# S5 blocks without zero halves, and products on 64x64 quarters of TensorE, in a hybrid layer

## Chip, cores and metric

One core of a Trainium2 chip runs the whole program. The metric is the device time of one execution in microseconds (us), median of several runs; lower is better.

## The reference

One layer on 512 positions of width 1024, all in float32. A normalised input goes through one projection `w_in`, whose columns feed three token mixers: A, sparse attention that keeps 128 keys a query; B, the S5 state space branch; C, a gated delta rule. Each is gated, projected and merged; then follow an output projection, a gated MLP with a short convolution and a last norm. The change lies in B alone:

```python
ab = exp(dt * (a_re + 1j * a_im))            # 32 groups x 64 states; here in complex form
bb = (ab - 1) / a * (b_re + 1j * b_im)       # 64 states x 16 channels a group
x  = einsum('tgm,gpm->tgp', u, bb)           # u: 512 positions, 32 groups of 16 channels
h[t] = ab * h[t-1] + x[t]
y  = einsum('tgp,gmp->tgm', h.re, c_re) - einsum('tgp,gmp->tgm', h.im, c_im) + d * u
y  = gelu(y);  y = y * sigmoid(y @ w_glu)
```

## The kernel before

**Chunks.** The sequence is cut in 128 chunks of 4 positions. For a group, its 16 channels by 4 positions j make 64 rows; two groups make a pair, so a pair's input is 128 rows by 128 chunks. `s5_uu` (L583) loads this input, U, from a copy `s_ud` in DRAM: a tile [128, 8, 128] for each half hf of 8 pairs, by 16 DMAs on SP's queue with 16 partitions each (L592).

**Tables.** `s5_setup` (L369) works out the powers of ab and bb on DVE, ACT and POOL. `s5_half` (L463), called for each half, builds the matrices of 8 pairs:
- `blocks` (L477 to L482) makes a tile of 128 x 8 x 128 and lets POOL set two of its quarters to zero (L480, L481): the blocks of a pair stand on the diagonal, since the groups don't mix.
- The B blocks (b4blk; L491 to L495), real and imaginary: a product u1 on DVE, a product u2 on POOL, and two combines of 64 partitions x 512 on DVE (L495), one for each group.
- kt (L501, L502): 16 products for 8 pairs, block x C with 16 columns moving. Transposes (L509) of the blocks, four to a PSUM bank, and copies by ACT (L510) give WT, which takes the input to the chunk's state.
- The CA blocks (cablk; L519 to L523) are made like the B blocks. kt and d give ks (L529, L530), which a product with the selection `selt` (L535) and two ACT copies (L539) turn into T, the part of the output that comes from the same chunk.
- The tables of cos and sin for the scan follow (L555 to L576).

**Steps.** `s5_main` (L596) then runs for each set of 4 pairs a state step A (`s5_state`, L647: 8 products WT x U into two banks `pt`, then a chain on DVE with two scans, which gives sr and si) and an output step B (`s5_out`, L692: 12 products T x U, CA0 x sr, CA1 x si into one bank `po`, gelu on ACT and DVE, and 8 DMAs of 16 partitions into `s_yd`, L715). The order is A0 A1 B0 A2 B1 A3 B2 B3. After these it loads the GLU weights (tiles glw), reads y back (yT, L618) and multiplies (L633 to L635).

**Helpers.** `mm` (L246) and `tr` (L249) record every product and transpose, so one line stands for all, and the tile names tell them apart. PSUM has the tags acc (2 banks), sm (2), pt (3) and po (1). `wload` (L271) brings 512 KB of weights (tile w, two buffers) through SP's queue, lets ACT cast the high part wh (L254) and DVE (L255), or for each third POOL (L284), subtract the low part wl; `dense` (L289) multiplies hh x wh, hl x wh and hh x wl. A float32 product of the program shows as two MATMUL and two LDWEIGHTS records, a transpose as one.

**Order.** S5 is a generator that yields between its parts. It is woven with a filler of projections (top-k part of A and the gates, in an order written out by hand) at a rate R_S5, and a scheduler then orders the instructions of each engine:

```python
fill = _order(ORD, {"t": tk, "g": gt})
drain(_weave(_chain(setup, self.s5_main()), fill, R_S5))
```

Of the kernel before, what the change touches and what calls it, by code (L numbers as in the profile page):

```python
# [50 lines left out]
def _consts():  # L51
# [25 lines left out]
    for g in range(2):  # L77
        for m in range(16):
            dm[g * 64 + 48 + m, m] = 1.0
# [9 lines left out]
def _layout(inp):  # L89
# [34 lines left out]
    pp("d", np.repeat(d, 4, 2).transpose(1, 2, 3, 0))  # L124
# [48 lines left out]
R_S5 = 1.075  # L173
R_QKV = 0.606
# [49 lines left out]
class _K:  # L224
# [238 lines left out]
    def s5_half(self, hf):  # L463
# [6 lines left out]
        dims = [128, 8, 4, 16]  # L470
        fl2 = lambda e: e.rearrange("p a b c d -> p a (b c d)")

        def b2t(nm):
            t = self.s5e.tile(dims, F32, tag="s2", name="s5_" + nm, bufs=2)
            return t

        def blocks(tag):  # L477
            e = (self.s5e if tag == "b4" else q).tile([128, 8, 2, 4, 16], F32, tag=tag, name="s5_" + tag + "blk", bufs={"b4": 4, "ca": 4, "T": 2}[tag])
            with self.tc.issue_after(self.lastp.ins):
                nc.gpsimd.memset(e[0:64, :, 1], 0.0)  # L480
                nc.gpsimd.memset(e[64:128, :, 0], 0.0)  # L481
            return e  # L482

        b4 = lambda a: _bc(a[:, sl], 2, 4)

        a4 = lambda a: _bc(a[:, sl, 3::-1], 3, 16)
        es = []
        for (x1, y1, x2, y2, op) in ((ar, bb[0], ai, bb[1], OP.subtract), (ar, bb[1], ai, bb[0], OP.add)):
            e = blocks("b4")
            u1, u2 = b2t("u1"), b2t("u2")  # L490
            tt(u1, a4(x1), b4(y1), OP.mult)  # L491
            (nc.gpsimd.tensor_tensor if 'u' in PO else tt)(u2, a4(x2), b4(y2), OP.mult)
            for g in range(2):
                s = slice(g * 64, g * 64 + 64)
                tt(e[s, :, g], u1[s], u2[s], op)  # L495
            es.append(e)
        cre3 = v3("cre")
        kt = self.acc("sm")
        for i in range(8):
            ko = kt[:, i * 16:i * 16 + 16]  # L500
            self.mm(ko, fl2(es[0])[:, i], cre3[:, hf * 8 + i], True, False)  # L501
            self.mm(ko, fl2(es[1])[:, i], cin[:, hf * 8 + i], False, True)  # L502
        WT = []
        for ri in range(2):
            w = q.tile([128, 8, 128], F32, tag="wt", name="s5_wt", bufs=4)
            for c in range(2):
                ps = self.acc("sm")
                for i in range(4):
                    self.tr(ps[:, i * 128:(i + 1) * 128], fl2(es[ri])[:, c * 4 + i])  # L509
                nc.scalar.copy(w[:, c * 4:c * 4 + 4].rearrange("p a b -> p (a b)"), ps)  # L510
            WT.append(w)
        yield 1

        a4 = lambda a: _bc(a[:, sl, 1:5], 3, 16)
        CA = []
        for ri, (y1, y2) in enumerate(((cre3, cin), (cin, cre3))):
            e = blocks("ca")
# [13 lines left out]
        T = blocks("T")  # L531
# [4 lines left out]
        pv = ps.rearrange("p (t a b) -> p a t b", t=4, a=8)  # L536
        for g in range(2):
            s = slice(g * 64, g * 64 + 64)
            nc.scalar.copy(T[s, :, g], pv[s])  # L539
# [55 lines left out]

    def s5_main(self):  # L596
        nc = self.nc
        self.yd = self.dp.tile([512, 512], F32, tag="yd", name="s5_yd", bufs=1)
        self.yyh, self.yyl, self.s5s_ = [], [], [None] * 4
# [3 lines left out]
        for st in ("A0", "A1", "B0", "A2", "B1", "A3", "B2", "B3"):  # L603
            qq = self.s5q[int(st[1])]
            if st[0] == "A":
                self.s5s_[int(st[1])] = self.s5_state(*qq)
            else:
                self.s5_out(*(qq[:5] + self.s5s_[int(st[1])]))
            yield 1
# [37 lines left out]
    def s5_state(self, hf, o, WT, CA, T, cosT, sinT, m4):  # L647
# [6 lines left out]
        pr_, pi_ = self.acc("pt"), self.acc("pt")  # L654
        for i in range(4):
# [36 lines left out]
    def s5_out(self, hf, o, WT, CA, T, sr, si):  # L692
        nc, q = self.nc, self.s5
        tt = nc.vector.tensor_tensor
        yv = self.yd.rearrange("(a g m) (t c) -> g t m a c", g=2, m=16, t=4)
        v = lambda x: x.rearrange("p (a c) -> p a c", a=4)
        qq = hf * 2 + o // 4
        U = self.U[hf]
        py = self.acc("po")
        for i in range(4):  # L700
            c = slice(i * 128, (i + 1) * 128)
            self.mm(py[:, c], T[:, o + i].rearrange("p g t m -> p (g t m)"), U[:, o + i], True, False)
            self.mm(py[:, c], CA[0][:, o + i], sr[:, i, 0:128], False, False)
            self.mm(py[:, c], CA[1][:, o + i], si[:, i, 0:128], False, True)
        s = q.tile([128, 512], F32, tag="b2", name="s5_gs", bufs=self.nb2)
        yy = q.tile([128, 512], F32, tag="b2", name="s5_yy", bufs=self.nb2)
        nc.scalar.activation(s, py, AF.Square)
        nc.vector.tensor_scalar(s, s, 0.044715, 1.0, OP.mult, OP.add)
        tt(s, s, py, OP.mult)
        nc.scalar.activation(s, s, AF.Tanh, scale=math.sqrt(2.0 / math.pi))  # L710
        nc.vector.scalar_tensor_tensor(yy, s, 1.0, py, OP.add, OP.mult)
# [911 lines left out]
```

## Time and profile before

| | |
|---|---|
| median of 3 runs | 957.44 us (954.11 to 960.42) |
| the profiled execution | 964.91 us |
| its span | 963.1 us, mean granted clock 0.981 |
| PE busy | 929.9 us (97%), 4572 records |
| DVE busy | 661.4 us (69%) |
| ACT, POOL busy | 418.2 us (43%), 138.6 us (14%) |

The span is the profiler's, from the first instruction to the last, and lies 1.8 us under that execution's time. Times in views are us from the span's start. Busy times of PE count overlapping records of pipelined products, so the time that a product costs is the distance of starts. S5's matrices are built from about 50 to 135 us and its steps run from 100 to 210 us, with the filler between them; the delta rule and the attention follow, and from some 600 us on the MLP.

### The profile page before, as it was taken

How to read it: one execution, taken by the hardware profiler on the slowest of the kernel's cores; microseconds unless marked ns; L12 is line 12 of the kernel's file. 1: busy time of each engine (PE TensorE's matmuls, PEld its weight loads, DVE VectorE, ACT ScalarE, POOL GpSimd, SP SyncE). 2: the span in 40 equal slices, each digit the busy share in tenths (PEclk: the TensorE clock that was granted, in tenths of full speed). 3: DMA queues.
4: the chain of work that ended last, by engine and by line, in shares of the span. 5: the costliest groups of instructions: out<-in, count | busy, mean ns of one | idle time of the engine just before them, and what ended most of it. 6: DMA issues, size and time to landing. Idle time of an engine off the chain costs nothing. (4 is left out here: it accounts for less than half of the span.)

```text
span 963.1 us, 12377 instructions
## 1 busy us (share of the span) xinstructions
PE 929.9 (97%) x4572; PEld 765.1 (79%) x4572; DVE 661.4 (69%) x1108; ACT 418.2 (43%) x751; POOL 138.6 (14%) x136
## 2 busy tenths in 40 slices
PE   7989999999999999899999999999999999999997
PEld 5668788788888787688867788988888888888885
DVE  5999779969998779436767746676766667622423
ACT  6455353335665643127861424444444443421312
POOL 3473403111123411302112000000000000000000
PEclk9999999999999999889999999999999999999999
DMA  8352513463224645523007542333232322223222
GB/s 317 123 154 88 141 67 100 151 186 108 87 91 116 175 120 164 152 69 141 23 23 241 187 173 73 125 97 100 89 109 88 107 90 94 103 88 110 88 65 88
DMA packets 54445, 113.49 MB, mean 118 GB/s; under 512 B 16240, under 2 KB 20720, under 8 KB 54384
## 3 DMA queue, kind: packets, MB, share of 16 engines
q1 hardware_dynamic: 52304, 109.28, 34.9%
q0 software_dynamic: 2080, 3.41, 1.9%
q8 instruction: 36, 0.59, 0.3%
q14 instruction: 25, 0.20, 0.1%
HBM read 94.84 MB, written 14.42 MB: 113 GB/s over the span
## 5 line engine op out<-in xcount | busy, mean ns | idle before, releaser
L255 DVE TENSOR_TENSOR wl<-w,wh 128x1024 fp32r<-128x1024 f32 (+1 forms) x121 | 147.8, 1222 | 130.8 <-ACT wh L254 130.6
L254 ACT CAST wh<-w 128x1024 fp32r<-128x1024 f32 (+1 forms) x121 | 125.3, 1036 | 187.5 <-PE ps_acc L246 80.9
L246 PE MATMUL ps_acc<-hh,wh 128*128 128x512 f32 x376 | 152.2, 405 | 4.7 <-ACT wh L254 2.9
L246 PE MATMUL ps_acc<-hh,wl 128*128 128x512 f32 x376 | 151.4, 403 | 3.3 <-DVE wl L255 3.3
L246 PE MATMUL ps_acc<-hl,wh 128*128 128x512 f32 x376 | 150.0, 399 | 0.0
L246 PEld LDWEIGHTS ps_acc<-hh,wh 128*128 128x128 f32 x376 | 72.4, 192 | 20.7 <-ACT wh L254 3.3
L246 PEld LDWEIGHTS ps_acc<-hh,wl 128*128 128x128 f32 x376 | 72.3, 192 | 20.4 <-DVE wl L255 4.5
L284 POOL TENSOR_TENSOR wl<-w,wh 128x1024 fp32r<-128x1024 f32 x19 | 53.4, 2809 | 222.9 <-ACT wh L283 161.0
L246 PEld LDWEIGHTS ps_acc<-hl,wh 128*128 128x128 f32 x376 | 72.1, 192 | 14.7
L246 PE MATMUL ps_acc<-f_hh,wh 128*128 128x512 f32 x160 | 62.3, 389 | 0.0
L246 PE MATMUL ps_acc<-f_hl,wh 128*128 128x512 f32 x160 | 62.3, 389 | 0.0
L246 PE MATMUL ps_acc<-f_hh,wl 128*128 128x512 f32 x160 | 62.3, 389 | 0.0
L246 PE MATMUL ps_sm<-f_hh,wh 128*128 128x512 f32 x160 | 62.3, 389 | 0.0
L246 PE MATMUL ps_sm<-f_hl,wh 128*128 128x512 f32 x160 | 62.3, 389 | 0.0
L246 PE MATMUL ps_sm<-f_hh,wl 128*128 128x512 f32 x160 | 62.3, 389 | 0.0
L335 POOL TENSOR_TENSOR frs<-rs,mhalf 128x1 f32<-128x1 f32 x4 | 2.2, 540 | 357.7 <-DVE rs L334 357.7
L254 ACT CAST ah<-f_th 128x512 fp32r<-128x512 f32 x22 | 13.6, 620 | 57.5 <-DVE f_th L1559 57.5
L246 PEld LDWEIGHTS ps_acc<-f_hl,wh 128*128 128x128 f32 x160 | 30.1, 188 | 6.3
L246 PEld LDWEIGHTS ps_sm<-f_hh,wh 128*128 128x128 f32 x160 | 30.1, 188 | 6.3
L246 PEld LDWEIGHTS ps_acc<-f_hh,wh 128*128 128x128 f32 x160 | 30.0, 188 | 6.3
L246 PEld LDWEIGHTS ps_sm<-f_hl,wh 128*128 128x128 f32 x160 | 30.0, 187 | 6.3
L246 PEld LDWEIGHTS ps_sm<-f_hh,wl 128*128 128x128 f32 x160 | 30.0, 188 | 6.2
(534 smaller groups left out, 2106.2 us busy)
## 6 DMA issues: line engine op xcount, KB each, us to landing
w<-in_w_in_dram SPq DMA_DIRECT2D x50, 512.0 KB, 3.7
w<-in_w_up_dram SPq DMA_DIRECT2D x44, 512.0 KB, 3.2
w<-in_w_down_dram SPq DMA_DIRECT2D x22, 512.0 KB, 3.2
gd<-m_th SPq DMA_DIRECT2D x24, 256.0 KB, 2.1
m_th<-gd SPq DMA_DIRECT2D x24, 256.0 KB, 3.3
w<-in_w_out_dram SPq DMA_DIRECT2D x8, 512.0 KB, 4.7
sq<-in_x_dram SPq DMA_DIRECT2D x4, 512.0 KB, 9.7
w<-in_w_proj_b_dram SPq DMA_DIRECT2D x4, 512.0 KB, 3.5
```

The costliest lines, as they stand in the source:

```text
L246: return self.nc.tensor.matmul(out, lhsT, rhs, start=start, stop=stop)
L254: self.lasta = nc.scalar.copy(hi, src)
L255: self.lastv = nc.vector.tensor_sub(lo, src, hi.bitcast(F32))
L284: nc.gpsimd.tensor_tensor(l[:, :n], w[:, :n], h[:, :n].bitcast(F32), OP.subtract)
L335: self.lastp = nc.gpsimd.tensor_tensor(dst, t[:, :width], self.mhalf[:, :width], OP.pow)
```

## The change

The two groups of a pair are no longer laid out as a diagonal of two blocks with zeros beside it. A tile of blocks holds only the blocks, 64 columns for each pair and part, the two groups in the two partition halves, and every product takes one 64x64 quarter of TensorE's array.

- **Blocks.** E [128, 8, 2, 64] holds real and imaginary B blocks side by side; CA is one tile of 1024 columns; T is [128, 8, 64]. The 20 memsets go. The first product is written straight into the tile and one combine of 128 partitions x 512, in place, follows. Tiles wt, ca and glw share a tag `big` with NBIG = 5 buffers. Within a block the order of channel m and step s is m*4+s, and `selt`, `dmask` and `d` follow.
- **Transposes.** 16 and not 32, since a 128x128 transpose now takes the real and imaginary block of two groups at once; 4 copies of WT by ACT for 8, and 2 of T (128x512) for 4 (64x512).
- **Input.** U is [128, 16, 128] for a half: the 64 rows of each of 16 groups stand in both partition halves, loaded by 4 DMAs of 64 partitions (512 KB each, 2 MB in all) in place of 16 of 64 KB (1 MB).
- **Products.** kt 32 for each half (16 before), WT 16 for each state step (8), outputs 48 for each half (24).
- **Steps.** A0 A1, output of half 0, A2 A3, output of half 1. The output of a half goes into two banks, one for each group of the pairs (po and one of pt), with gelu on both in two parts; 8 DMAs of 64 partitions write y (32 of 16). The GLU's input y_hl takes the buffers of U.
- Lines of helpers move: `mm` is L247, `tr` L250, the cast L255, wl L256, U's DMAs L577.

The core of the diff:

```diff
-            e = blocks("b4")
-            u1, u2 = b2t("u1"), b2t("u2")
-            tt(u1, a4(x1), b4(y1), OP.mult)
+            e, u2 = ms(E[:, :, ri]), u2t("u2")
+            tt(e, a4(x1), b4(y1), OP.mult)
             (nc.gpsimd.tensor_tensor if 'u' in PO else tt)(u2, a4(x2), b4(y2), OP.mult)
-            for g in range(2):
-                s = slice(g * 64, g * 64 + 64)
-                tt(e[s, :, g], u1[s], u2[s], op)
-            es.append(e)
+            tt(e, e, u2, op)
         cre3 = v3("cre")
+
         kt = self.acc("sm")
         for i in range(8):
-            ko = kt[:, i * 16:i * 16 + 16]
-            self.mm(ko, fl2(es[0])[:, i], cre3[:, hf * 8 + i], True, False)
-            self.mm(ko, fl2(es[1])[:, i], cin[:, hf * 8 + i], False, True)
...
+            for ri, c3 in ((0, cre3), (1, cin)):
+                for r in rows:
+                    self.mm(kt[r, i * 16:i * 16 + 16], E[r, i, ri], c3[r, hf * 8 + i], ri == 0, ri == 1)
...
+        v = self.ud.rearrange("(h b m) (j c) -> h (m j) b c", h=2, m=16, j=4)
         for hf in range(2):
-            U = self.s5.tile([128, 8, 128], F32, tag="U", name="s5_U", bufs=2)
-            for g in range(2):
-                for j in range(4):
-                    b = (g * 4 + j) * 16
-                    nc.sync.dma_start(U[b:b + 16], v[g][j][:, hf * 8:hf * 8 + 8])
+            U = self.s5.tile([128, 16, 128], F32, tag="U", name="s5_U", bufs=2)
+            for r in range(2):
+                nc.sync.dma_start(U[r * 64:r * 64 + 64], v[hf])
...
         for i in range(4):
             c = slice(i * 128, (i + 1) * 128)
-            self.mm(pr_[:, c], WT[0][:, o + i], U[:, o + i])
-            self.mm(pi_[:, c], WT[1][:, o + i], U[:, o + i])
+            for g in range(2):
+                for p_, r in ((pr_, rows[0]), (pi_, rows[1])):
+                    self.mm(p_[rows[g], c], WT[r, o + i, rows[g]], U[r, (o + i) * 2 + g])
...
+        py = (self.acc("po"), self.acc("pt"))
+        for i in range(0, 8, 2):
+            (sr, si), k = S[i // 4], i % 4
+            for z in range(3):
+                for a2 in range(2):
+                    for g in range(2):
+                        r = rows[g]
+                        w = (T, CA[0], CA[1])[z][r, i + a2]
+                        x = (U[r, (i + a2) * 2 + g], sr[r, k + a2, 0:128], si[r, k + a2, 0:128])[z]
+                        self.mm(py[g][rows[a2], i * 64:i * 64 + 128], w, x, z == 0 and i == 0, z == 2 and i == 6)
+        yield 1
```

In the order of TensorE's instructions, this is the place where WT's products of the first state steps and kt of the second half stand between projections (ikl, a_iq: index keys of A; hh, hl, wh, wl: a projection). Before:

```order
L246 MATMUL ps_sm<-ikl,a_iq 128x512
L246 MATMUL ps_acc<-hh,wl 128x512
L246 MATMUL ps_pt<-s_U,s_wt 128x128 x7
L246 MATMUL ps_po<-s_U,s_Tblk 128x128
L246 MATMUL ps_sm<-par,s_b4blk 128x16 x16
L249 MATMUL ps_sm<-ident,s_b4blk 128x128 x4
L246 MATMUL ps_acc<-hh,wh 128x512
```

The same place in the kernel with the change:

```order
L247 MATMUL ps_sm<-ikl,a_iq 128x512
L247 MATMUL ps_acc<-hl,wh 128x512
L247 MATMUL ps_acc<-hh,wl 128x512
L247 MATMUL ps_pt<-s_U,s_wt 64x128 x11
L247 MATMUL ps_sm<-par,s_b_875 64x16 x32
L250 MATMUL ps_sm<-ident,s_b_875 128x128 x4
L247 MATMUL ps_acc<-hh,wh 128x512
```

Quarter products stand in a row here, 11 and 32, between full ones; the product of T has left this place, as the output comes later. In the whole order there are 16 such groups of quarter products between full ones.

In SP's order of DMA issues, this is the place of U's loads, behind the last store of `s_ud`, with weight loads (w) and stores of the filler (gd) behind. Before:

```order
L1409 DMA s_ud<-sq 128x512
L274 DMA w<-in_w_in_dram 128x1024
L592 DMA s_U<-s_ud 16x8x128 x16
L1264 DMA gd_486<-m_th 128x512
L274 DMA w<-in_w_in_dram 128x1024 x2
L1264 DMA gd_532<-m_th 128x512
```

The same place in the kernel with the change:

```order
L1405 DMA s_ud<-sq 128x512
L275 DMA w<-in_w_in_dram 128x1024
L577 DMA s_U<-s_ud 64x16x128 x4
L275 DMA w<-in_w_in_dram 128x1024
L1260 DMA gd_474<-m_th 128x512
L275 DMA w<-in_w_in_dram 128x1024
L1260 DMA gd_520<-m_th 128x512
```

Four issues stand where 16 stood, and the first weight load has moved ahead of the store that stood between them.

## Rows read from the trace of the kernel before

**Rows 1.** The page: busy time of each engine with its share of the span and its number of instructions, and the granted clock of TensorE in 40 equal slices of the span, in tenths of full speed (9 is 90% or more).

```profile
PE 929.9 (97%) x4572; PEld 765.1 (79%) x4572; DVE 661.4 (69%) x1108; ACT 418.2 (43%) x751; POOL 138.6 (14%) x136
...
PEclk9999999999999999889999999999999999999999
```

**Rows 2.** Windows of the span: stretch, its length, busy time (and instructions) of PE, PEld, DVE, ACT and POOL, then the granted clock of TensorE, the busy share of the DMA engines and the GB/s they moved.

```profile
60.00:65.00 5.00, 2.31 (x11) 1.55 (x9) 4.83 (x12) 0.87 (x1) 1.18 (x1) 1.00 0.99 318
62.30:66.70 4.40, 0.88 (x4) 0.45 (x4) 4.37 (x7) 2.37 (x3) 1.18 (x1) 1.00 0.59 233
66.70:70.10 3.40, 3.40 (x9) 2.64 (x10) 3.35 (x4) 1.51 (x2) 2.86 (x2) 0.50 0.75 210
179.30:182.70 3.40, 3.40 (x10) 2.66 (x9) 3.40 (x7) 1.04 (x1) 0.03 (x1) 0.50 0.83 264
40.00:100.00 60.00, 52.45 (x250) 41.66 (x248) 58.06 (x99) 32.68 (x43) 29.79 (x33) 0.97 0.37 110
220.00:300.00 80.00, 80.00 (x375) 65.86 (x374) 79.97 (x168) 50.39 (x127) 12.70 (x6) 1.00 0.29 93
```

**Rows 3.** Waits of PE between 60 and 215 us: what waited, for what, us in total, times, the longest.

```profile
PE ps_acc L246 <- ACT wh L254: 2.9, 1, 2.9
PE ps_acc L246 <- DVE wl L255: 2.8, 2, 2.2
PE ps_acc L246 <- DVE sp_l L266: 1.8, 1, 1.8
```

**Rows 4.** Timeline of SP's DMA issues, 50 to 68 us: start, length, line, transfer, how many.

```profile
50.72 7.43 SPq L592 DMA_DIRECT2D s_U<-s_ud  x16
...
58.73 0.93 SPq L274 DMA_DIRECT2D w<-in_w_in_dram  x2
```

**Rows 5.** Timeline of ScalarE, 58 to 67 us; in brackets the idle time before and what ended it.

```profile
64.13 1.05 ACT L254 CAST wh<-w 128x1024 fp32r<-128x1024 f32 x1 [4.33 <-DMA w<-in_w_in_dram]
```

**Rows 6.** Timeline of PE, 61 to 67.2 us.

```profile
61.91 0.40 PE L246 MATMUL ps_acc<-hh,wl 128*128 128x512 f32 x1
65.22 0.50 PE L246 MATMUL ps_acc<-hh,wh 128*128 128x512 f32 x1 [2.92 <-ACT wh L254]
...
66.55 0.69 PE L246 MATMUL ps_acc<-hh,wl 128*128 128x512 f32 x1 [0.60 <-DVE wl L255]
```

**Rows 7.** Timeline of PE, 115 to 121.2 us. A row of several records has the start of the first and the end of the last.

```profile
115.34 1.72 PE L246 MATMUL ps_pt<-s_U,s_wt 128*128 128x128 f32 x14
116.89 0.39 PE L246 MATMUL ps_po<-s_U,s_Tblk 128*128 128x128 f32 x2
117.12 3.64 PE L246 MATMUL ps_sm<-par,s_b4blk 128*128 128x16 f32 x32
120.61 0.63 PE L249 MATMUL ps_sm<-ident,s_b4blk 128*128 128x128 f32 x4
121.00 0.52 PE L246 MATMUL ps_acc<-hh,wh 128*128 128x512 f32 x1
```

**Rows 8.** Groups of instructions by line and shape: xcount | busy us, mean ns of one | idle before. PE's three, DVE's combine of the B blocks, POOL's clearing of the CA blocks (one of its lines; the others have the same shape).

```profile
L246 PE MATMUL ps_pt<-s_U,s_wt 128*128 128x128 f32 x64 | 8.9, 280 | 0.0
...
L246 PE MATMUL ps_sm<-par,s_b4blk 128*128 128x16 f32 x64 | 7.4, 259 | 0.0
...
L495 DVE TENSOR_TENSOR s_b4blk<-s_u,s_u 64x512 f32<-64x512 f32 x8 | 6.2, 776 | 0.1
L246 PE MATMUL ps_po<-s_U,s_Tblk 128*128 128x128 f32 x32 | 6.2, 275 | 0.0
...
L480 POOL MEMSET s_cablk<- 64x512 f32 x4 | 2.4, 596 | 0.1
```

**Rows 9.** Timeline of PE, 437.9 to 438.7 us: products of the delta rule, whose two operands lie in two opposite 64x64 quarters.

```profile
437.95 0.50 PE L246 MATMUL ps_sm<-g_Y,g_P 64*64 64x64 f32 x5
438.24 0.27 PE L246 MATMUL ps_sm<-g_X,g_NT 64*64 64x64 f32 x1
438.29 0.22 PE L246 MATMUL ps_sm<-g_Y,g_P 64*64 64x64 f32 x1
438.34 0.22 PE L246 MATMUL ps_sm<-g_X,g_NT 64*64 64x64 f32 x1
438.35 0.22 PE L246 MATMUL ps_sm<-g_Y,g_P 64*64 64x64 f32 x1
438.40 0.22 PE L246 MATMUL ps_sm<-g_X,g_NT 64*64 64x64 f32 x1
438.41 0.22 PE L246 MATMUL ps_sm<-g_Y,g_P 64*64 64x64 f32 x1
438.46 0.45 PE L246 MATMUL ps_sm<-g_X,g_NT 64*64 64x64 f32 x5
```

**Rows 10.** Timeline of PE, 503.6 to 505.8 us: half-width products of the attention between full ones.

```profile
503.86 0.40 PE L246 MATMUL ps_acc<-g_oh,wl 128*128 128x512 f32 x1
504.10 0.39 PE L246 MATMUL ps_acc<-g_oh,wh 128*128 128x512 f32 x1
504.42 1.09 PE L246 MATMUL ps_po<-a_pT,a_V 128*64 128x128 f32 x14
505.44 0.50 PE L246 MATMUL ps_acc<-g_ol,wh 128*128 128x512 f32 x1
505.77 0.40 PE L246 MATMUL ps_acc<-g_oh,wl 128*128 128x512 f32 x1
```

More of the change, by code (lines that the diff above doesn't have):

```diff
@@ L78, in _consts @@
         for m in range(16):
[L79 removed]
+            dm[g * 64 + m * 4 + 3, m] = 1.0
     put("dmask", dm)
@@ L173 @@
 R_S5 = 1.075
+NBIG = 5
 R_QKV = 0.606
@@ L530, in s5_half @@
         tt(ks, kt[:, :128].rearrange("p (a b) -> p a b", a=8), u, OP.add)
-        T = blocks("T")
+        T = q.tile([128, 8, 64], F32, tag="T", name="s5_T", bufs=2)
         selt = self.selt
@@ L535, in s5_half @@
             self.mm(ps[:, t * 128:(t + 1) * 128], selt[:, t * 128:(t + 1) * 128], ks.rearrange("p a b -> p (a b)"))
[L536 to L539, printed above, removed]
+        nc.scalar.copy(ms(T), ps.rearrange("p (t a b) -> p a b t", t=4, a=8))
         yield 1
@@ L602, in s5_main @@
             yield from self.s5_half(hf)
[L603 to L609, printed above, removed]
+        for hf in range(2):
+            S = []
+            for o in range(2):
+                S.append(self.s5_state(*self.s5q[hf * 2 + o]))
+                yield 1
+            yield from self.s5_out(*(self.s5q[hf * 2][:5] + (S,)))
         glu = []
         for n2 in range(2):
-            hl = [self.s5.tile([128, 1024], F32R, tag="wt", name="s5_glw", bufs=4) for _ in range(2)]
+            hl = [self.s5.tile([128, 1024], F32R, tag="big", name="s5_glw", bufs=NBIG) for _ in range(2)]
             self.wload(self.I["w_glu"][n2], hl=hl)
@@ L690, in s5_state, with s5_out @@
         return sr, si
-    def s5_out(self, hf, o, WT, CA, T, sr, si):
+    def s5_out(self, hf, o, WT, CA, T, S):
         nc, q = self.nc, self.s5
         tt = nc.vector.tensor_tensor
-        yv = self.yd.rearrange("(a g m) (t c) -> g t m a c", g=2, m=16, t=4)
-        v = lambda x: x.rearrange("p (a c) -> p a c", a=4)
-        qq = hf * 2 + o // 4
+        yv = self.yd.rearrange("(h b a g m) (t c) -> h g a (m t) b c", h=2, a=2, g=2, m=16, t=4)
         U = self.U[hf]
[L699 to L711, printed above, removed]
-        for g in range(2):
-            for t in range(4):
-                b = (g * 4 + t) * 16
-                nc.sync.dma_start(yv[g][t][:, qq * 4:qq * 4 + 4], v(yy)[b:b + 16])
@@ new lines, in s5_out @@
+        yield 1
+        for g in range(2):
+            s = q.tile([128, 512], F32, tag="b2", name="s5_gs", bufs=self.nb2)
+            yy = q.tile([128, 512], F32, tag="b2", name="s5_yy", bufs=self.nb2)
+            nc.scalar.activation(s, py[g], AF.Square)
+            nc.vector.tensor_scalar(s, s, 0.044715, 1.0, OP.mult, OP.add)
+            tt(s, s, py[g], OP.mult)
+            nc.scalar.activation(s, s, AF.Tanh, scale=math.sqrt(2.0 / math.pi))
+            nc.vector.scalar_tensor_tensor(yy, s, 1.0, py[g], OP.add, OP.mult)
+            for a2 in range(2):
+                nc.sync.dma_start(yv[hf][g][a2], yy[rows[a2]].rearrange("p (b c) -> p b c", b=4))
+            if g == 0:
+                yield 1
```

66 lines of the change are left out of this document (30 added, 36 removed).

## The prediction

> **What bounds the kernel now.** I read the page's busy times first: PE is busy 929.9 us of a 963.1 us span, DVE 69% and POOL 14% [rows 1]. The program ends when PE is done, so an edit pays only if it shortens PE's work, shortens a wait of PE's, or gives PE's clock back. The line of the granted clock says where the last of these can be: it is at full speed but for two slices in the middle [rows 1], and shorter falls disappear in the slices' means.
>
> Next come the stages by windows [rows 2]. The branch that changes (S5) is woven with projections between 40 and 200 us. In 40 to 100 us DVE works 58.06 of 60 us and PE 52.45, so PE has gaps there and DVE is nearly full. In 220 to 300 us, behind S5, PE and DVE are both full (80.00 and 79.97 of 80): what PE gains earlier lasts only if DVE comes earlier by as much.
>
> PE's waits between 60 and 215 us name few causes: 2.9 us for the cast wh, 2.8 us for wl (two waits) and 1.8 us for sp_l [rows 3]. The first is an effect of S5's own loads. SP issues the 16 DMAs of U from 50.72 on for 7.43 us, and the weight load behind them is issued only at 58.73 [rows 4]. The cast of that weight had waited 4.33 us for the load when it began at 64.13 [rows 5]. PE's product at 61.91 is followed by one at 65.22 (idle 2.92) and one at 66.55 (idle 0.60) [rows 6]. While PE does 0.88 us of work in 4.40 the clock is 1.00, and in the 3.40 us after that it is 0.50: 1.2 GHz in place of 2.4 [rows 2]. There are four such stretches of 3.40 us at 0.50 in S5's part; the first and the last are shown. Each does 1.7 us of full-speed work, so each costs 1.7 us.
>
> **The products.** PE's own time is read from starts in the trace, since busy times of pipelined records overlap. In fp32 each product of the program shows as two records. Fourteen WT records take 115.34 to 116.89, 0.111 us each; 32 kt records, with 16 columns only, 117.12 to 120.61, 0.109 each; four transposes 120.61 to 121.00, 0.098 each [rows 7]. So a 128x128 block costs 0.11 whether 128 columns move or 16. There are 64 WT, 64 kt and 96 output records (T with 32, CA twice with 32) [rows 8] (the two CA groups are like T's): 7.1 + 7.0 + 10.6 = 24.7 us. After the change there are twice as many, 448, each on a 64x64 quarter, and neighbours in the order lie in different quarters.
>
> No quarters of this kind, 64 rows by 64 columns with 128 columns moving, stand in the trace. The nearest are the products g_Y and g_X, two opposite quarters with 64 columns moving [rows 9]. Five g_Y records alone go from 437.95 to 438.24, 58 ns each; from 438.29 to 438.46 records of both quarters start alternately, six in 0.17 us, 28 ns each. So two quarters do run at the same time, and a record takes half as long. For 128 columns the record alone would be 0.11, in pairs 0.055, and with all four quarters filled 0.028. WT and the outputs fill four in rotation; kt fills two diagonal ones with 16 columns moving, where the weights set the time, 58 ns alone and 28 in pairs. I take 0.030 for all 448, which is nearest to the 28 of the overlap: 13.4 us, that is 11.3 less than before. The ends are 0.027 (12.6 less) and 0.11, no overlap (49 us, 25 more for all; for kt 58 ns is the end of its own, which leaves +21). The 16 transposes that go in two halves give 1.6 us: together -12.9.
>
> Against this stand the switches. When a group of half-width products (a_pT,a_V) comes between full ones, the last full one starts at 504.10 and the next at 505.44; less the pace of 0.24 (503.86 to 504.10) and 14 records by 0.055, 0.33 us are left over [rows 10]. The full product after it takes 0.33 to the next rather than 0.24, but that is paid after any group of short products, in the old form too. The order puts the quarter products in 16 groups: 16 x 0.33 = 5.3, less about 0.8 for old groups that go. Bounds: 0 and 16 x 0.44 = 7. PE net: -12.9 + 4.5 = -8.4.
>
> The page "TensorEngine Tiling (Array Packing)" of the Trainium skill, Key Properties, has a rule that speaks against the change: a new tiling mode first drains the array. The 0.33 us of rows 10 agrees in sign; by the rule the switch is paid per group, which is how I count it, and a planner that scattered the quarters singly would lose the gain.
>
> **The loads of U.** SP now issues 4 DMAs where it issued 16, and the next weight load stands right behind. At 0.46 us each (7.43 / 16) [rows 4], or twice that for larger ones, that is 2 to 4 us in place of 7.4, so w is issued at 53 to 55 and not 58.7. But U now stands twice: 2 MB for 1 MB. The stretch 60 to 65 moved 318 GB/s [rows 2], at which 2 MB take 6.6 us, and from 51 on they end at 58, w behind them at 60 if the rate holds; if the 512-byte pieces run at half that, at 65 as before. I take 61 to 62: 2 to 3 us of the 3.5 us of stall go, and with a gap that short the half-speed stretch behind it too (1.7): -4.2. Bounds: +1 (the double bytes are later than now) and -5.2. What is late next is DVE's wl, on which the second idle of 0.60 already hangs.
>
> **DVE, POOL, ACT.** The blocks' combines were 16 instructions on 64 partitions, mean 0.776 for the first kind [rows 8]; now 8 on 128 partitions with the same 512 elements each. I give DVE -5.5 us, in 60 to 110 us where it is full; bounds -5 and -8 (the second kind has longer means). POOL loses 20 memsets by 0.5 to 0.6 [rows 8], 11 us, on an engine at 14%; only through the shared work of POOL and DVE on u could it be felt, and I count 0, bounds 0 and -1. ACT loses 4 copies of WT and two of T, some 3.5 us of an engine at 43%: 0. yd's 32 writes become 8, which takes SP's queue from ahead of weight loads around 180 us; the wait for wl of 2.2 us there may go or not.
>
> DVE's 5.5 us pay where PE waits for wl or sp_l (2.8 + 1.8) and in the three later half-speed stretches (5.1): I count 3 of the 9.7. On the other side PE, 8 us shorter, catches up with DVE sooner, and from 220 us on DVE is full: what PE is ahead by more than DVE gives back there, as waits or as clock. I count +4 for it, bounds 0 and +8.
>
> **The sum.** -8.4 - 4.2 - 3 + 4 = -11.6, say -12 us against the profiled execution of 964.91 us (span 963.1), 953. That execution lies 7.5 over the median of the runs, 957.44, and the change is set off against the median: **946 us**. About 1% (9.6 us) is what a measurement of this kernel can tell from no change.
>
> **Rivals.**
> - *Only two quarters overlap* (0.055 a record): 448 by 0.055 is 24.6, as before; PE's net is -1.6 + 4.5 = +3, the loads and DVE give -7, and less comes back later: about 953. For it: two at a time is all that rows 9 show. Against it: the two do so without any loss, and nothing in them is at a limit.
> - *DVE bound* in 220 to 300 keeps all but DVE's own 5.5 and the early stall's part: about 951. For it: 79.97 of 80 [rows 2]. Against: PE too is full there, so some of the waiting is mutual.
> - *The double U* holds w back as the issues did: stall and slow clock stay, -8.4 - 3 + 4, about 950; for it the 0.50 clock and 318 GB/s seen around 60 to 70 us.
> - *A cost per record.* If every record took a fixed time at the sequencer near the 50 ns that the 16 g_Y and g_X records average (437.95 to 438.46, and the last five at 58 ns), 448 records take 22 and not 13 us, 9 more: 955. The 28 ns of the alternating starts [rows 9] speak against it. The Trainium skill's "TensorE: Matmul & The Clock Gate", in the section on the back-to-back issue gap, gives about 62 ns an instruction; if that were per record, it would be 27.8 us in all, and the time 957 to 961, but rows 9 show records closer than that.
> - *Slower*: the quarter products of WT and the outputs don't overlap, because each one reads its 64 rows of weights and data through a path that the next one shares. Place: the WT and output groups at 100 to 200 us. At 0.11 a record they cost 35 us for 17.7; with kt and transposes -5 and +4.5 for the switches PE gains +17, less 7 for loads and DVE and with nothing given back later: 967 to 969. It decides from about 0.08 us a record on. Against it: rows 9 again.
>
> **Chances.** Forecast 0.50 (its own range 938 to 951), better still (four quarters at 0.027, all stalls gone) 0.07, two quarters 0.13, DVE bound 0.10, double U 0.08, cost per record 0.06, slower 0.06. Some 0.35 of the forecast's 0.50 lies under 947.9 (1% faster), with 0.07 of the better case and 0.09 of the four rivals between: faster 0.51, slower 0.06, within 1% 0.43. The range takes in the rivals up to the cost per record and leaves the slower case and the skirts outside: 936 to 958.
>
> **What would show it.** Right: 32 WT records in about 1 us and 64 kt records in 2 us; gaps of some 0.33 us at the groups' edges; the weight load after U issued by 55 us, no PE wait over 1 us before 66 us and the clock at 1.00 in 66 to 70. DVE shorter by 5 us in 40 to 110. Wrong: records spaced 0.055 or 0.11; a wait of PE for wh at 60 to 68 that stays; more half-speed stretches in 100 to 300; PE reaching 220 us earlier by 12 but 300 us by much less. If the runs come at 955 or more while the records are at 0.030, the switches or DVE have taken the gain.

## The result: slower by 1.2%, and the profile after

| | before | after |
|---|---|---|
| median of 4 runs each | 958.93 us (954.11 to 960.70) | 969.31 us (966.99 to 970.28) |
| ratio, 95% interval | 1 | 1.0118 (1.0077 to 1.0159) |
| profiled execution (span) | 964.91 us (963.1) | 970.28 us (967.8) |

The forecast was 946 us. The two profiled executions stand only 5.4 us apart, as the one of before lies 6 us over its median. The page of the kernel with the change, busy times and clock (against [rows 1]):

```profile
PE 920.6 (95%) x4780; PEld 747.8 (77%) x4780; DVE 647.7 (67%) x1100; ACT 414.8 (43%) x745; POOL 124.2 (13%) x116
...
PEclk9988999998999999989999999999999999999999
```

PE, DVE, ACT and POOL are all busy for less time than before; the execution is longer. So the loss is time in which PE does nothing. PE's waits from 40 to 320 us (against [rows 3], which reach from 60 to 215 us):

```profile
PE ps_acc L247 <- ACT m_th L1259: 9.3, 2, 7.4
PE ps_acc L247 <- ACT g_raw L753: 6.0, 1, 6.0
PE ps_acc L247 <- DVE wl L256: 4.1, 2, 2.8
PE ps_sm L247 <- DMA a_iq<-sp_l: 2.2, 1, 2.2
PE ps_sm L247 <- ACT a_rel L1061: 2.0, 1, 2.0
PE ps_po L247 <- DVE s_sr L674: 2.0, 2, 1.2
...
```

Two single waits stand out, 7.4 us for an eviction m_th and 6.0 us for g_raw. Neither tile belongs to S5: m_th holds gates of the filler, g_raw a projection of the delta rule, and ACT writes both from PSUM banks (it evicts them). Windows of the span, with the columns of [rows 2]:

```profile
40.00:100.00 60.00, 46.60 (x244) 35.77 (x243) 48.31 (x91) 27.44 (x35) 20.33 (x20) 0.89 0.51 127
64.70:71.50 6.80, 3.29 (x8) 2.62 (x9) 2.10 (x6) 6.21 (x8) 0.00 (x0) 0.50 0.57 202
...
235.30:242.20 6.90, 6.15 (x15) 4.80 (x16) 5.48 (x12) 6.05 (x11) 0.00 (x0) 0.51 0.21 83
```

In 40 to 100 us PE is busy 46.60 us where it was 52.45, and DVE 48.31 where it was 58.06. PE comes out of both waits (at 68.21 and 236.05, below) inside a stretch of some 7 us at 1.2 GHz, twice as long as the 3.40 us of [rows 2]. It has products running in 3.29 and 6.15 us of the two, and half of that is what the clock costs there.

**The books.** From the starts and ends of all products in a trace, I added up the time in which no product ran (idle, by stretch) and the time at a granted clock of 0.50 in which products ran (slow). Work is the end of the last product less idle and less half of slow, so it is what PE does at full speed. All in us, one execution each (the kernels below the second line are explained with their experiments):

| | idle 40-100 | 100-205 | 205-300 | rest | slow | end | work |
|---|---|---|---|---|---|---|---|
| before | 7.5 | 2.2 | 0 | 16.6 | 34.1 | 956.2 | 912.9 |
| after | 13.4 | 7.2 | 6.0 | 13.6 | 28.4 | 960.7 | 906.4 |
| a_pt | 12.8 | 6.9 | 2.3 | 15.1 | 28.6 | 955.8 | 904.5 |
| a_ptv | 8.8 | 5.8 | 2.3 | 15.9 | 11.4 | 944.5 | 906.0 |
| a_w3 | 7.9 | 4.3 | 0.1 | 13.9 | 24.2 | 942.9 | 904.6 |
| b_v | 5.9 | 2.6 | 0 | 14.5 | 27.3 | 948.8 | 912.1 |

Work fell by 6.5 us (forecast 8.4), and half of slow by 2.9. Idle rose by 13.9: 5.9 early, 5.0 while S5's steps run, 6.0 behind S5, less 3 elsewhere. -6.5 - 2.9 + 13.9 = +4.5, the distance of the two ends.

**Where the quarters pay.** PE's timeline around kt and around WT (against [rows 7]):

```profile
92.08 2.04 PE L247 MATMUL ps_sm<-par,s_b 64*64 64x16 f32 x64
94.05 0.66 PE L250 MATMUL ps_sm<-ident,s_b 128*128 128x128 f32 x4
...
164.30 0.39 PE L247 MATMUL ps_acc<-hl,wh 128*128 128x512 f32 x1
164.53 0.40 PE L247 MATMUL ps_acc<-hh,wl 128*128 128x512 f32 x1
164.86 1.10 PE L247 MATMUL ps_pt<-s_U,s_wt 64*64 64x128 f32 x32
165.89 0.50 PE L247 MATMUL ps_acc<-hh,wh 128*128 128x512 f32 x1
166.23 0.39 PE L247 MATMUL ps_acc<-hl,wh 128*128 128x512 f32 x1
```

64 kt records in 94.05 - 92.08 = 1.97 us are 31 ns each, 32 WT records in 1.03 us are 32 ns: the 30 of the forecast, for 16 columns moving on two quarters and for 128 on four. That the two agree doesn't mean that issuing sets the pace. The output's records alternate between banks and so have rows of their own:

```profile
151.08 0.27 PE L247 MATMUL ps_pt<-s_sr,s_ca 64*64 64x128 f32 x1
...
151.10 0.27 PE L247 MATMUL ps_po<-s_si,s_ca 64*64 64x128 f32 x1
151.19 0.27 PE L247 MATMUL ps_pt<-s_sr,s_ca 64*64 64x128 f32 x1
```

Four of them start within 0.02 us, and the next four 0.11 us after the first: records start far closer together than 31 ns, and each quarter goes on at the 0.11 of a 128x128 record [rows 7]. The starts of kt come as pairs, one pair in 0.058 us, the time of a record in one quarter alone in [rows 9].

The last full product ahead of WT takes 0.33 to the next start at a pace of 0.23, so the way in costs 0.10, and the way out (165.89 to 166.23) 0.11. A short group costs more for its size:

```profile
104.22 0.44 PE L247 MATMUL ps_pt<-s_U,s_wt 64*64 64x128 f32 x4
104.59 0.50 PE L247 MATMUL ps_acc<-hh,wl 128*128 128x512 f32 x1
```

Four records alone take 0.37 us, where four at 31 ns would take 0.12. Added up from starts, without waits and with the ways in and out, the 448 quarter records take 19.2 us and the 224 records that they replace 24.2 to 24.6, by how their ways in and out are counted: 5.0 to 5.4 less.

**Where it goes, first place: U's loads.** SP's issues from 48 to 59 us (against [rows 4]), ScalarE from 60 to 68 (against [rows 5]), PE from 60 to 69 (against [rows 6]):

```profile
48.78 4.87 SPq L577 DMA_DIRECT2D s_U<-s_ud  x4
53.74 4.24 SPq L275 DMA_DIRECT2D w<-in_w_in_dram  x1
...
58.56 0.38 SPq L275 DMA_DIRECT2D w<-in_w_in_dram  x1
```

```profile
65.20 1.04 ACT L255 CAST wh<-w 128x1024 fp32r<-128x1024 f32 x1 [9.25 <-DMA w<-in_w_in_dram]
66.27 1.28 ACT L1259 ACT_TABLE_LOAD   x1
67.56 0.60 ACT L1259 ACTIVATE m_th<-ps_acc 128x512 f32<-128x512 f32 x1
```

```profile
60.39 0.40 PE L247 MATMUL ps_acc<-hh,wl 128*128 128x512 f32 x1
68.21 0.79 PE L247 MATMUL ps_acc<-hh,wh 128*128 128x512 f32 x1 [7.42 <-ACT m_th L1259]
```

The weight load is issued 5 us earlier than before, at 53.74, as forecast. But its issue now holds SP for 4.24 us, where the next but one takes 0.38, and the cast that waits for it begins at 65.20, later than before (64.13). On ACT the eviction m_th stands behind that cast, with a table load of 1.28 us between; PE needs the PSUM bank which m_th empties, so PE waits 7.42 us. Before, the order on ACT was another: the m_th of that place stood ahead of the cast of 64.13.

```profile
59.20 0.60 ACT L1263 ACTIVATE m_th<-ps_acc 128x512 f32<-128x512 f32 x1
```

So the wait is 4.5 us longer than the 2.92 of [rows 6] in three parts. PE runs dry 1.5 us earlier (its last product starts at 60.39, before at 61.91). The cast begins 1.1 us later. And from the cast's begin to PE's next product pass 3.0 us and not 1.1, as m_th and its table load stand between. What turned ACT's order here is not shown. The transfers of 48 to 66 us by queue (KB each, median us from issue to landing):

```profile
DMA packets 4723, 3.61 MB, mean 201 GB/s; under 512 B 130, under 2 KB 4226, under 8 KB 4723
...
s_U<-s_ud SPq DMA_DIRECT2D x4, 512.0 KB, 9.4
w<-in_w_in_dram SPq DMA_DIRECT2D x2, 512.0 KB, 10.0
```

The stretch, with U's 2 MB in 512-byte pieces, moves 201 GB/s and not the 318 of [rows 2], and a w lands some 10 us behind its issue. While U moves, the DMA engines are as busy as in the stretch of 318, 0.98 for 0.99, and move little more than half (the last two figures):

```profile
48.80:58.00 9.20, 9.20 (x43) 7.23 (x42) 9.16 (x30) 7.06 (x10) 2.76 (x4) 1.00 0.98 171
```

**Second place: g_raw.** PE and ACT around 230 us:

```profile
229.66 0.39 PE L247 MATMUL ps_acc<-hh,wl 128*128 128x512 f32 x1
236.05 0.80 PE L247 MATMUL ps_acc<-hh,wh 128*128 128x512 f32 x1 [6.00 <-ACT g_raw L753]
```

```profile
230.81 1.13 ACT L628 ACTIVATE s_bo<-s_gl 128x512 f32<-128x512 f32 x1
...
233.97 1.11 ACT L628 ACTIVATE s_bo<-s_gl 128x512 f32<-128x512 f32 x1 [1.61 <-DVE s_gl L624]
234.88 0.64 ACT L751 ACTIVATE g_k<-ps_acc,cw 128x512 f32<-128x512 f32 x1
235.43 0.57 ACT L753 COPY g_raw<-ps_acc 128x512 f32<-128x512 f32 x1
```

The delta rule's first evictions, g_k and g_raw, stand behind all of S5's gate activations (s_gl, s_bo) on ACT; PE waits for one of the banks acc. Before, the first g_k stood ahead of the first s_gl, and PE did not wait:

```profile
218.18 0.68 ACT L755 ACTIVATE g_k<-ps_acc,cw 128x512 f32<-128x512 f32 x1
...
220.38 0.60 ACT L637 ACTIVATE s_gl<-ps_pt 128x512 f32<-128x512 f32 x1 [1.04 <-PE ps_pt L246]
```

Nothing in the diff touches these instructions. What it does touch is memory: the tile y_hl of S5's end now shares the buffers of U. In the built kernel it takes bytes 101,728 to 109,920 of each partition, and g_v of the delta rule bytes 95,584 to 103,776: 2,048 bytes are in both.

### The profile page after: what moved, and what is told of

Its sections match the earlier page's. It is cut to its first block, busy times and chain, and to the rows that moved or that the text cites. A ratio compares the mean times of both kernels' runs of the same rounds, so it can differ in the third digit from the quotient of the medians.

```text
span 967.8 us, 12691 instructions
## 1 busy us (share of the span) xinstructions
PE 920.6 (95%) x4780; PEld 747.8 (77%) x4780; DVE 647.7 (67%) x1100; ACT 414.8 (43%) x745; POOL 124.2 (13%) x116
## 5 line engine op out<-in xcount | busy, mean ns | idle before, releaser
L256 DVE TENSOR_TENSOR wl<-w,wh 128x1024 fp32r<-128x1024 f32 (+1 forms) x121 | 147.1, 1217 | 144.7 <-ACT wh L255 144.6
L255 ACT CAST wh<-w 128x1024 fp32r<-128x1024 f32 (+1 forms) x121 | 125.5, 1038 | 197.9 <-PE ps_acc L247 86.5
L247 PE MATMUL ps_acc<-hh,wh 128*128 128x512 f32 x376 | 153.5, 408 | 15.3 <-ACT m_th L1259 9.3
L247 PE MATMUL ps_acc<-hh,wl 128*128 128x512 f32 x376 | 152.0, 404 | 4.5 <-DVE wl L256 4.5
L247 PE MATMUL ps_acc<-hl,wh 128*128 128x512 f32 x376 | 150.1, 399 | 0.0
L247 PEld LDWEIGHTS ps_acc<-hh,wh 128*128 128x128 f32 x376 | 72.6, 193 | 32.0 <-ACT m_th L1259 10.2
L247 PEld LDWEIGHTS ps_acc<-hh,wl 128*128 128x128 f32 x376 | 72.4, 192 | 23.0 <-DVE wl L256 6.1
L247 PEld LDWEIGHTS ps_acc<-hl,wh 128*128 128x128 f32 x376 | 72.7, 193 | 15.5 <-issue 0.5
L285 POOL TENSOR_TENSOR wl<-w,wh 128x1024 fp32r<-128x1024 f32 x19 | 50.8, 2673 | 233.0 <-ACT wh L284 201.5
L247 PE MATMUL ps_acc<-f_hh,wh 128*128 128x512 f32 x160 | 62.3, 389 | 0.0
L247 PE MATMUL ps_acc<-f_hl,wh 128*128 128x512 f32 x160 | 62.3, 389 | 0.0
L247 PE MATMUL ps_acc<-f_hh,wl 128*128 128x512 f32 x160 | 62.2, 389 | 0.0
L247 PE MATMUL ps_sm<-f_hh,wh 128*128 128x512 f32 x160 | 62.2, 389 | 0.0
L247 PE MATMUL ps_sm<-f_hl,wh 128*128 128x512 f32 x160 | 62.2, 389 | 0.0
L247 PE MATMUL ps_sm<-f_hh,wl 128*128 128x512 f32 x160 | 62.2, 389 | 0.0
L255 ACT CAST ah<-f_th 128x512 fp32r<-128x512 f32 x22 | 13.6, 620 | 57.6 <-DVE f_th L1555 57.6
L247 PEld LDWEIGHTS ps_sm<-f_hh,wh 128*128 128x128 f32 x160 | 30.1, 188 | 6.3
L247 PEld LDWEIGHTS ps_acc<-f_hl,wh 128*128 128x128 f32 x160 | 30.1, 188 | 6.2
L247 PEld LDWEIGHTS ps_acc<-f_hh,wl 128*128 128x128 f32 x160 | 30.1, 188 | 6.2
L247 PEld LDWEIGHTS ps_sm<-f_hh,wl 128*128 128x128 f32 x160 | 30.0, 188 | 6.2
L247 PEld LDWEIGHTS ps_acc<-f_hh,wh 128*128 128x128 f32 x160 | 30.0, 187 | 6.3
```

What stands on the lines that cost most here:

```text
L247: return self.nc.tensor.matmul(out, lhsT, rhs, start=start, stop=stop)
L255: self.lasta = nc.scalar.copy(hi, src)
L256: self.lastv = nc.vector.tensor_sub(lo, src, hi.bitcast(F32))
L285: nc.gpsimd.tensor_tensor(l[:, :n], w[:, :n], h[:, :n].bitcast(F32), OP.subtract)
```

## Experiments

Theories: (U) the doubled loads of U hold up a weight load, and PE behind it; (M) the shared 2,048 bytes turn ACT's order round; (G) DVE, full behind S5, takes PE's gain back whatever happens earlier. (G) is the rival, the forecast's "+4". Ratios are to the kernel before on the same chip. Names with a_ are the kernel with the change, b_ the kernel before, each with the edit shown.

**a_pt and a_pad: 2 KB between.** a_pt puts an unused tile under U; a_pad gives the tag of u2 a third buffer, which moves U and y_hl by the same 2 KB.

```python
+        if hf == 0:                                               # a_pt, in s5_half
+            pd = self.s5e.tile([128, 512], F32, tag="pd", name="s5_pd", bufs=1)
+            nc.gpsimd.memset(pd[:, :4], 0.0)
...
-    t = self.s5e.tile(dims, F32, tag="s2", name="s5_" + nm, bufs=2)
+    t = self.s5e.tile(dims, F32, tag="s2", name="s5_" + nm, bufs=3)   # a_pad
```

> The changed kernel with one size changed: u2 has three buffers, not two, which moves the tiles of U and y_hl up by 2 KB, so that the delta rule's g_v no longer lies over y_hl; in the order the first copies of g_k and g_raw on ScalarE then stand ahead of the GLU's activations and not behind them. Theory M (memory): PE's wait of 6.0 us for g_raw at 230 to 236 goes, and the half-speed stretch of 6.8 us behind it (3.4 us lost); 969 becomes 959 to 962. Rival D (DVE is full there, so the wait only moves): PE waits as long somewhere in 220 to 300, 967 to 970.

> The changed kernel with a tile of 2 KB that is not used ahead of the B blocks, in place of u2's third buffer in a_pad: the place of the tiles alone. ScalarE's order is the changed kernel's up to the GLU and there the kernel before's (y_hl four times, g_k, then the GLU's). Theory M: PE's wait of 6.0 us for g_raw goes, with the slow stretch behind it, and 969 becomes 959 to 963, as with a_pad (962). Rival B (u2's third buffer made a_pad's gain): 967 to 970.

Measured: a_pad 961.94 us, 1.0017 (0.9988 to 1.0046); a_pt 961.91, 1.0031 (1.0003 to 1.0059). Both intervals lie under that of the change as it is. ScalarE in a_pt:

```profile
217.07 0.68 ACT L754 ACTIVATE g_k<-ps_acc,cw 128x512 f32<-128x512 f32 x1
217.65 0.57 ACT L756 COPY g_raw<-ps_acc 128x512 f32<-128x512 f32 x1
218.12 0.61 ACT L626 ACTIVATE s_gl<-ps_pt 128x512 f32<-128x512 f32 x1
```

g_k and g_raw are ahead of s_gl again, 18 us earlier, and PE's wait for g_raw is gone. (M) holds: a shift by 2 KB, made in two ways, is worth some 7 us by the medians. The 7.4 us for m_th stays in a_pt, as (U) wants.

**a_v, b_v, a_vpad, a_ptv: U's loads later.** The loads of a half are issued when that half is built; half 0 stays ahead of the weight load, half 1 goes behind four more. b_v does the same to the kernel before (8 of its 16 DMAs); a_vpad is a_v with a_pad's edit, a_ptv with a_pt's.

```python
-                nc.sync.dma_start(U[r * 64:r * 64 + 64], v[hf])
+                self.ul.append((hf, U[r * 64:r * 64 + 64], v[hf]))
...
+    def s5_ul(self, hf):                   # called in s5_half(hf), ahead of CA
+        with self.tc.issue_after(self.lastw.ins):     # the last weight load so far
+            for h, dst, src in self.ul:
+                if h == hf:
+                    self.nc.sync.dma_start(dst, src)
```

> The changed kernel with the loads of U for the second half moved in SP's order behind four more weight loads, so that 1 MB and not 2 MB stand ahead of the weight load at 53 us. Theory U (the bytes of the double input hold that load back): it lands 4 to 6 us earlier than at 65.2, PE's wait of 7.4 us shrinks to under 3, a half-speed stretch of 6.8 us becomes 3.4 or none; 969 becomes 960 to 965. Rival S (the time is lost to S5's own chain on DVE, and the weights are only what PE waits for by chance): PE waits elsewhere before 125 us and the time stays within 3 us of 969.

> The kernel before with the same move of U's second half (8 of its 16 DMAs) behind four weight loads: a control for the gain of a_v. Its own early stall (2.9 + 0.6 us and a half-speed stretch) goes in part: 959 becomes 954 to 958. If it gains as much as a_v does, the double input was not what cost the changed kernel its time.

> Both edits. If M and U hold and are independent the gains add: 969 becomes 949 to 956, under the kernel before (959). If the quarter products themselves cost more than they save (rival Q: switches of the array's mode, more records), both waits go and the time stays at 959 or above.

> The same tile, and U's second half behind four weight loads (as in a_vpad). Both theories: 954 to 960, as a_vpad (959), and within 3 us of b_v (957): the quarter products still give nothing at the end.

Measured: a_v 964.39, 1.0049 (1.0020 to 1.0078); a_vpad 959.09, 0.9976 (0.9949 to 1.0004); a_ptv 954.84, 0.9976 (0.9942 to 1.0010); b_v 956.63, 0.9968 (0.9931 to 1.0006). The two edits make a square of ratios: neither 1.0118, the shift alone 1.0017 or 1.0031, the later loads alone 1.0049, both 0.9976 in either form. The wait for m_th shrinks where the loads are later, though ACT's order there stays as it is; in a_ptv:

```profile
59.93 0.50 PE L247 MATMUL ps_acc<-hh,wh 128*128 128x512 f32 x1 [2.25 <-ACT m_th L1269]
```

Idle 40-100 goes from 12.8 (a_pt) to 8.8 (a_ptv), and slow in 40 to 205 us from 15.1 to 11.4. In 300 to 955 us slow goes from 13.5 to 0, which nothing ties to U's loads. So (U) holds for the wait. By the runs it is weaker: later loads gain 0.4 to 0.7% in the three pairs, the control b_v 0.3% on before at the edge of its interval, so that 0.1 to 0.4% is left for the doubled input alone, with intervals that overlap. a_vpad missed its range (949 to 956) and came at the number of its rival, by which the products cost more than they save. Against that rival stands its work, 908.1, still 4.8 us under before.

**a_w3: later still.** As a_ptv, but half 0 too goes behind two more weight loads.

```python
+        self.s5_ul(hf)                     # moved here, ahead of the scan's tables
         cb = _bc(self.C("cidx"), 1, 4)
```

> a_ptv with U's first half moved as well, behind two more weight loads, so that nothing of the double input stands ahead of the weight load at 50 us; PE's and ScalarE's order around the GLU as in a_ptv. Theory U: PE's idle time in 40 to 100 us falls from 8.8 to 4 to 7, and the median from 954.8 to 949 to 953, 0.6 to 1.1% under the kernel before. Rival C (in that stretch S5's chain on DVE and ScalarE is what PE waits for, whatever the loads do): the idle time moves within 40 to 100 us and the median stays at 953 to 957.

Measured: 953.10 (948.11 to 958.87), 0.9952 (0.9923 to 0.9980). SP's issues and PE's waits in that stretch:

```profile
51.37 0.33 SPq L275 DMA_DIRECT2D w<-in_w_in_dram  x1
51.75 1.62 SPq L589 DMA_DIRECT2D s_U<-s_ud  x2
...
57.74 0.33 SPq L275 DMA_DIRECT2D w<-in_w_in_dram  x1
```

```profile
70.33 0.50 PE L247 MATMUL ps_acc<-hh,wh 128*128 128x512 f32 x1 [1.76 <-ACT m_th L1269]
...
73.83 0.80 PE L247 MATMUL ps_acc<-hh,wl 128*128 128x512 f32 x1 [2.77 <-DVE wl L256]
```

Two DMAs of U alone issue in 1.62 us, the weight loads around them in 0.33, and the wait for m_th is 1.76. This version beats both kernels, by 0.5% over the one before; it is not told apart from a_ptv or b_v. Against its expectation idle 40-100 (7.9, for 4 to 7) and the median (for 949 to 953) lie just outside theory U's ranges, and the median lies in rival C's (953 to 957): what is still idle there hangs on more than the loads, such as the 2.77 us for wl.

**b_dbl: the double bytes alone.** The kernel before, with two more DMAs of 512 KB in 512-byte pieces behind U's, into a DRAM tile that nothing reads.

```python
+        X = self.dp.tile([2, 64, 16, 128], F32, tag="X", name="s5_X", bufs=1)
+        w = self.ud.rearrange("(h b m) (j c) -> h (m j) b c", h=2, m=16, j=4)
+        for hf in range(2):
+            with self.tc.issue_after(last.ins):       # last: the last DMA of U
+                nc.sync.dma_start(X[hf], w[hf])
```

> The kernel before, with 1 MB more read from s_ud in 512-byte pieces behind U's loads, by two DMAs of 512 KB to a DRAM tile that nothing reads. Theory U (bytes and pieces ahead of the weight load are what held it back): the weight load behind lands 4 to 7 us later than at 64.1, PE's wait of 2.9 us becomes 7 to 10; 959 becomes 962 to 968. Rival I (the issue of DMAs on SP's queue, not the bytes, holds it): two issues more, 1 to 2 us, and the time stays within 2 us.

Measured: 963.62, 1.0043 (1.0014 to 1.0073). ScalarE's cast and PE's longest wait:

```profile
66.97 1.04 ACT L254 CAST wh<-w 128x1024 fp32r<-128x1024 f32 x1 [4.58 <-DMA w<-in_w_in_dram]
```

```profile
67.69 0.58 PE L246 MATMUL ps_sm<-par,s_b4blk 128*128 128x16 f32 x2 [5.93 <-issue]
```

1 MB more at this place makes the kernel before slower by 0.4%, with no quarter product in it. The cast moves from 64.13 to 66.97, 2.8 us and not the 4 to 7 expected. The wait of 5.93 us is not for the weight: kt stands ahead of the projection in PE's order here, and PE goes on just when DVE ends the B blocks' combine, at 67.59.

```profile
65.46 2.13 DVE L495 TENSOR_TENSOR s_b4blk<-s_u,s_u 64x512 f32<-64x512 f32 x2
```

The cast ends at 68.01, so that the projection could have gone on hardly earlier. Idle in 40 to 100 us is 7.5 us as before, since other waits there are shorter; how the runs come to 5 us more is not shown.

**a_tt, b_t: DVE relieved behind S5.** a_ptv and b_v with 8 of the 16 rounds in the top-k part left out, so that 64 keys a query stay and not 128: DVE has less to do, and the output is another.

```python
         for rd in range(16):
-            for qt in (3, 2, 1):
+            for qt in (3, 2, 1) if rd < 8 else ():
```

> a_ptv with the first 8 of the 16 rounds of the top-k left out on DVE (64 keys stay and not 128), some 25 us less of DVE's work between 150 and 300 us. Theory G (the products' gain is lost because DVE is full behind S5): with DVE relieved the changed kernel leads b_t by 5 to 10 us. Rival N (the products' gain was never there, or something else holds the delta rule's start): a_tt and b_t within 3 us, as a_ptv and b_v are.

> b_v with the same 8 rounds left out; its ScalarE has the same order around the GLU as a_tt. By theory G it gains less than a_ptv does from the same edit, since PE was busy all through 200 to 300 in b_v: 945 to 955, and a_tt 940 to 948.

Measured: a_tt 955.27, 0.9969 (0.9940 to 0.9998); b_t 960.18, 1.0020 (0.9991 to 1.0049). Windows of 205 to 300 us, in the order a_ptv, a_tt, b_v, b_t (third busy time: DVE):

```profile
205.00:300.00 95.00, 92.67 (x428) 75.80 (x427) 94.52 (x202) 56.35 (x137) 16.39 (x7) 1.00 0.28 90
```

```profile
205.00:300.00 95.00, 94.16 (x433) 76.87 (x432) 75.97 (x128) 53.92 (x133) 17.75 (x12) 1.00 0.30 99
```

```profile
205.00:300.00 95.00, 95.00 (x441) 78.14 (x440) 94.97 (x206) 56.89 (x138) 16.14 (x7) 1.00 0.30 103
```

```profile
205.00:300.00 95.00, 95.00 (x436) 77.94 (x435) 77.19 (x132) 54.82 (x134) 14.53 (x8) 1.00 0.32 104
```

DVE falls from 95 to 76 or 77 us. By (G) a_tt was to come at 940 to 948 and to lead b_t by 5 to 10 us. It came at 955, no faster than a_ptv, as b_t is no faster than b_v; PE's idle time there falls from 2.3 to 0.8 us in a_tt, which the medians don't show. a_tt does lead b_t by 4.9 us, between the 5 of (G) and the 3 of rival N, but since b_t is slower than b_v by 3.6 and not since a_tt gained; why b_t is slower is not shown. So (G) falls as the cause of the loss: a DVE that is relieved gives nothing back.

**a_g2, b_g2: subtractions of wl to POOL.** a_vpad and b_v with each second weight, not each third, subtracted on POOL once S5 is over.

```python
-        if self.gpw and GP and self.wi % GP == 0:
+        if self.gpw and GP and self.wi % self.gpn == 0:    # GP (3) in S5, 2 afterwards
```

> The changed kernel with both edits of a_vpad, and from the end of S5 on every second low part wl of the weights on POOL, not every third, which takes DVE's work down where DVE is full (200 to 300 us). Theory G (what S5 gains is given back because DVE is full there): PE keeps the 9 us that it is ahead at 200 us, its waits for wl after 200 us go, and 959 becomes 950 to 954. Rival P (PE's own order or its clock takes it back): under 2 us of gain.

> The same edit of wl in the kernel before with U's second half moved (b_v). PE is busy all through 200 to 300 there and waits for nothing, so theory G has it at 955 to 958, as b_v. If it gains as much as a_g2 does, DVE bounded both, and the edit tells nothing of the change.

Measured: a_g2 957.08, 0.9968 (0.9938 to 0.9998); b_g2 968.59, 1.0122 (1.0067 to 1.0177). This tells nothing of (G). DVE is as busy in 205 to 300 us as without the edit (a_g2 94.92 us, a_vpad 93.59). And in b_g2 the weight loads on SP wait 17.6 us for POOL's wl in 300 to 400 us, where none does in b_v, and PE's idle time there goes from 4.5 to 8.3. b_g2 missed its 955 to 958, a_g2 its 950 to 954. A relief that doesn't reach the engine is no test of it; the two before it are cleaner.

## Why the prediction was wrong

- **What bounds the kernel** was read rightly: the time followed PE's waits.
- **The products** came as forecast: 31 to 32 ns for 30. So the rivals "only two quarters overlap", "a cost per record" and "slower", which all need longer records, were out at once. The median, 969.31, lies next to the 967 to 969 of *Slower*, but by a mechanism that none of the rivals names: that is chance. Two slips bear on nothing: no overlap with kt at 58 ns makes +18 and not +21, and [rows 9] have five and not six steps in the 0.17 us (half of the 58 ns is 29 all the same).
- **The switches** were about right as a sum, and not as 0.33 on each group: long groups cost less (0.10 us in, and little more than 31 ns a record), groups of four 0.25 beyond their records. Quarters and switches were to take 13.4 + 4.5 = 17.9 us for 24.7; they took 19.2 for 24.2 to 24.6. The transposes gave 1.7 (forecast 1.6), and PE's work fell 6.5 us for the forecast 8.4. The Trainium skill's rule that a new tiling mode drains the array ("TensorEngine Tiling (Array Packing)", Key Properties) agrees in sign with the 0.10 us.
- **The loads of U are the step that failed: -4.2 us, bounds +1 and -5.2.** I took SP's queue for the bottleneck and w for landed at 61 to 62 us. In the trace w is issued by 55 us as the step says, but that issue itself takes 4.24 us and its bytes queue behind 2 MB in small pieces (in the trace the last of U lands at 64.1 us and w at 65.1), by the worse of the two rates that I weighed. Idle in 40 to 100 us rose by 5.9. The bound of +1 was wrong for a second reason: I weighed only the cast, and not what is queued behind it on ACT. The eviction m_th, and through its bank PE, hung on the same load; of the 4.5 us by which the wait grew, 1.1 are the later cast and 1.9 the m_th behind it. a_ptv and a_w3 give most of it back (idle 8.8 and 7.9); that the doubled bytes alone cost as much is not shown, since b_dbl is 5 us slower but its trace doesn't tie them to the weight. The rival "double U" had the mechanism, but priced it at no more than the loss of the gain: a_pt, with this loss and without the next, came at 962, not at 950.
- **DVE, POOL, ACT: -3.** DVE's busy time fell 13.7 us in all, but waits for wl did not shrink (from 40 to 320 us 2.8 before, 4.1 now), and slow in 40 to 205 us went from 13.7 only to 12.0, 0.8 us for PE. Little of the -3 shows.
- **The give-back, +4.** PE, earlier, did run into others, by 5.0 us of idle, but at 100 to 205 us in S5's scan (s_sr, s_si: 2.9 us of waits) and in the filler's part A (a_iq, a_rel: 4.2), not behind S5 on DVE. The size was about right, the place and the cause were wrong; the rival "DVE bound" went with it (a_tt, b_t). No run was aimed at these 5.0 us; in a_pad the waits of part A are gone, and its median is a_pt's.
- **Missed: where a tile lies.** y_hl in U's buffers looked like a change of names. The sum has no term for it. It cost a wait of 6.00 us and 3.1 for the clock behind it, some 7 us by a_pt and a_pad. That the order turns because of the overlap itself is read from the addresses; shown is that 2 KB undo it.

So by the parts: the forecast's -11.6 becomes -6.5 (work) - 2.9 (clock) + 5.9 (U) + 5.0 (S5's steps) + 6.0 (g_raw) - 3 (idle elsewhere) = +4.5 between the two profiled executions. The medians differ by 10.4, as before's profiled one lies 6 over its median; what those 6 are is not shown.

Open: with both losses taken out, work is 7.5 us less than in b_v (912.1 to 904.6) while the medians of a_w3 and b_v, from two chips, differ by 3.5 us, inside their intervals. Idle in all is 3.2 us more in a_w3 (26.2 to 23.0) and half of slow 1.6 less, so the ends of the two traces differ by 5.9; the rest is within what runs differ by. U in larger pieces wasn't tried.

## What to carry to other kernels

When loads are merged into fewer issues, count bytes and pieces too, and follow the load behind them to its end: through the cast that waits for it to every eviction queued behind that cast. When a tile moves to another buffer, compare the order of all engines far behind the change, since a tile that shares a few bytes with a later one can turn a queue round. And when a change shortens the bounding engine and the time doesn't follow, add up idle and slow time by stretch before blaming the next busiest engine: DVE at 95 of 95 us gave nothing back here when it was relieved.

## What the runs showed of the hardware

- An issue on SP can last long when much is still on its way: a weight load's took 4.24 us behind 2 MB of U (4.28 in a_pt), 0.77 right behind 1 MB of it (a_v), and 0.33 behind 1 MB with 4 us between (a_w3).
- DMA engines that are busy 0.98 of the time moved 171 GB/s while U went in 512-byte pieces, and 318 at 0.99 in the stretch of [rows 2].
- Quarter products with 16 columns moving on two quarters and with 128 on four take the same in long groups, 31 and 32 ns a record; on four quarters they start in fours, 0.11 us apart, on two in pairs, 0.058 us apart.
- The way into a long group of quarter products cost 0.10 us and the way out 0.11; a group of four records alone took 0.37 us between them.
